# One product of 512 columns for both parts of the activations, and a norm output that is rebuilt

## The chip, the cores and the metric

One core of a Trainium2 chip runs the whole program. Its engines work side by side, each through its own queue in order: TensorE (PE, with PEld for the load of the stationary operand), VectorE (DVE), ScalarE (ACT), GpSimd (POOL), and SyncE (SP), which issues the DMAs. They wait for each other through semaphores. The metric is the device time of one execution in microseconds.

## The reference, cut to what matters

Two layers on 256 tokens of width 1024. Layer 0 mixes tokens by a convolution module, layer 1 by attention; each is followed by an MLP. Every sub-layer starts from a norm with a scale and a shift that come from the conditioning vector c:

```python
h = rms_norm(x, mix_norm_g[i]) * (1.0 + sc1) + sh1
y = conformer_conv(h, ...) if i % 2 == 0 else moba_attention(h, ...)
x = x + g1 * y
h = rms_norm(x, mlp_norm_g[i]) * (1.0 + sc2) + sh2
x = x + g2 * (jnp.square(jax.nn.relu(h @ mlp_w1[i])) @ mlp_w2[i])
```

The hidden width of the MLP is 4096; attention has 16 heads of 64. The modulation vectors (sh, sc, g) are products of silu(c) with ada_w, 6 x 1024 columns for each layer.

## The kernel before, in words

Activations stand transposed: 128 channels on the partitions, 256 tokens along the row, KT = 8 such tiles for the width 1024. Every operand of a large product is kept as two fp32r parts, high and low. For weights, `split` loads 1 MB (`raw`, 5 buffers), rounds it on ACT to `wh`, and subtracts on DVE (in layer 0 a quarter on POOL) to get `wl`; both have 3 buffers. `mm3` then makes a step of three products into the same PSUM region: wh by the high activations, wh by the low ones, wl by the high ones, 256 columns each. A step stands for one tile of 128 output channels and 128 input channels.

The norm is not applied ahead of the products. `norm_prep` stores xT * gm (gm is g * (1 + scale)) in xh and xl, unnormalised. Two more columns (NE = 258) hold the shift, so that a product's column 256 is the shift's share. The token factors `rs_ext` (one over the root mean square) come later, while the products already run, and `evict` multiplies them in when it takes a result out of PSUM; the share of the shift is then added as a bias by ACT (`finish` in the MLP, `squares` and `values` in attention).

An MLP (`mlp(l, slots)`) runs `six` first: w1's blocks b = 0 to 2 (a block is 256 output channels, 16 steps), whose results wait for the token factors. Then come blocks b = 3 to 15, each with `w1_split(b)`, 16 steps and two `finish`. `finish` is a relu and two squares on ACT and one subtraction on DVE into sh and sl. The product with w2 takes 4 column blocks by 4 pieces of the inner width, 16 steps each, and adds the result times the gate to xT on DVE.

The PE's order is written out by hand; short pieces of other work (columns sums, transposes, attention scores) are placed by counting steps (`tick`, `at`). The other engines' queues are set by a scheduler when the program is built: it takes what the program gives it in order, and lets a later instruction pass an earlier one that has to wait. In layer 0 and in the middle of the program DVE also multiplies ada_w by silu(c) (`ada_dve`, `ada_a` in the rows: 4 instructions for each MB of weights).

Attention (`Heads`) takes qkv by blocks of 4 heads, b = 0 to 3, with z = 0, 1, 2 for q, k, v. Block 0 runs in `six`; during block 1 the heads of block 0 go through sums of squares, `norms` (a chain of short DVE instructions that ends with `rb`), `keys` (`kb`, transposes on PE) and the scores.

Of the kernel before, what the change touches and what calls it, by code (L numbers as in the profile page):

```python
# [30 lines left out]
def trunk(ctx, tc, x, c, ada_w, ada_b, mix_g, mlp_g, w_in, b_in, dw, dw_b, ln_g, ln_b, w_out, b_out,
# [123 lines left out]
    xh = const.tile([P, KT, NE], F32R, name="xh")  # L155
    xl = const.tile([P, KT, NE], F32R, name="xl")
    pool.memset(xh[:, :, S:].bitcast(F32), 0.0)
    pool.memset(xl[:, :, S:].bitcast(F32), 0.0)
# [661 lines left out]
    def mlp(l, slots):  # L820

        def fill():
# [3 lines left out]
        with tc.tile_pool(name=f"mlp{l}", bufs=1) as mp:  # L826
            sh = mp.tile([P, FF // P, S], F32R, name="sh")
            sl = mp.tile([P, FF // P, S], F32R, name="sl")
            def finish(ps, f):
# [3 lines left out]
                act.activation(s, t[:, :S], AF.Relu, bias=t[:, S:S + 1])  # L833
                act.activation(sh[:, f, :], s, AF.Square)
                act.activation(s, s, AF.Square)
                dve.tensor_sub(sl[:, f, :], s, sh[:, f, :].bitcast(F32))
# [266 lines left out]
```

## Time and profile before

| what | value |
|---|---|
| median of 3 runs | 672.47 us (672.23 to 672.62) |
| the profiled execution | 670.39 us, its span 668.6 us |
| PE busy | 654.0 us, 98% of the span |
| DVE busy | 494.2 us, 74% |
| ACT busy | 369.2 us, 55% |
| POOL busy | 125.6 us, 19% |
| bytes moved | 150.07 MB, mean 224 GB/s |

The span runs from the first to the last instruction; the profiled execution took 1.8 us more than its span, and 2.1 us less than the median of the runs. PE's busy time is the union of overlapping products whose ends are modelled, so it says where PE had work, not how fast it went. For its speed one reads when products start.

### The profile page before, as it was taken

The page shows a single profiled execution, that of the slowest core. Times are in us where ns is not written, and L with a number is a line of the kernel's source. Part 1 is how long each engine was busy: PE and PEld are TensorE (multiplying, and loading weights), DVE is VectorE, ACT ScalarE, POOL GpSimd, SP SyncE. Part 2 cuts the span into 40 slices and gives each one's busy share as a digit, 9 for nine tenths or more (in the row PEclk, how much of TensorE's full clock was granted, in tenths as well). Part 3 has the DMA queues.
Part 4 walks back from the last instruction along what each step waited for, and adds up shares of the span by engine and source line. Part 5 has one row for each costly group of instructions (what it writes and reads, how often), then busy time and mean ns, then how long its engine had stood idle before and what let it go on. Part 6 is the DMA issues. An engine that isn't in the chain of part 4 may idle for free.

```text
span 668.6 us, 14398 instructions
## 1 busy us (share of the span) xinstructions
PE 654.0 (98%) x5909; PEld 605.2 (91%) x5909; DVE 494.2 (74%) x924; ACT 369.2 (55%) x678; POOL 125.6 (19%) x167
## 2 busy tenths in 40 slices
PE   7899999999999999999999999999999999999997
PEld 6777866699999999999999988988899999999997
DVE  3647993567799999999974998887769986544440
ACT  4537443385877676334443567566668777533330
POOL 5461042302333323345420000000200000000000
PEclk9999999999999999999999999999999999999999
DMA  8998609586479989999994733533356995555300
GB/s 302 340 351 295 240 2 373 216 251 211 151 250 336 346 278 349 342 349 336 349 337 130 237 97 112 181 123 105 101 169 205 334 293 191 186 188 178 110 17 17
DMA packets 107871, 150.07 MB, mean 224 GB/s; under 512 B 2871, under 2 KB 91120, under 8 KB 107806
## 3 DMA queue, kind: packets, MB, share of 16 engines
q1 hardware_dynamic: 107310, 149.04, 66.4%
q8 instruction: 46, 0.75, 0.5%
q14 instruction: 19, 0.16, 0.1%
q0 software_dynamic: 352, 0.07, 0.1%
q10 hardware_dynamic: 144, 0.06, 0.0%
HBM read 148.10 MB, written 1.05 MB: 223 GB/s over the span
## 4 chain that ended last, share of the span: by engine, by line
PE 68%; DVE 21%; issue 4%; ACT 3%; POOL 2%; DMA 2%; SPq 1%; DVEq 0%; ACTq 0%; POOLq 0%
PE m L208 11%; PE m L210 11%; PE m L209 11%; DVE ada_a L301 8%; DVE wl L199 7%; PE qkv L208 4%; PE qkv L209 3%; PE qkv L210 3%; PE cv L403 3%; PE ko L209 2%; PE ko L208 2%; PE ci L208 2%; PE ko L210 2%; PE rep L393 2%; PE ci L210 2%
## 5 line engine op out<-in xcount | busy, mean ns | idle before, releaser
L199 DVE TENSOR_TENSOR wl<-raw,wh 128x1024 fp32r<-128x1024 f32 (+2 forms) x176 | 204.5, 1181 | 59.0 <-ACT wh L196 57.8
L196 ACT CAST wh<-raw 128x1024 fp32r<-128x1024 f32 x176 | 177.7, 1043 | 107.0 <-PE m L209 58.8
L210 PE MATMUL m<-xh,wl 128*128 128x258 f32 x512 | 144.5, 282 | 1.2 <-DVE wl L199 1.1
L208 PE MATMUL m<-sh,wh 128*128 128x256 f32 x512 | 145.4, 284 | 0.0
L210 PE MATMUL m<-sh,wl 128*128 128x256 f32 x512 | 144.3, 282 | 0.8 <-DVE wl L199 0.8
L208 PE MATMUL m<-xh,wh 128*128 128x258 f32 x512 | 145.1, 283 | 0.0
L209 PE MATMUL m<-xl,wh 128*128 128x258 f32 x512 | 144.7, 283 | 0.0
L209 PE MATMUL m<-sl,wh 128*128 128x256 f32 x512 | 144.0, 281 | 0.0
L210 PEld LDWEIGHTS m<-xh,wl 128*128 128x128 f32 x512 | 96.7, 189 | 1.8 <-DVE wl L199 1.8
L208 PEld LDWEIGHTS m<-sh,wh 128*128 128x128 f32 x512 | 96.4, 188 | 1.6 <-issue 0.8
L210 PEld LDWEIGHTS m<-sh,wl 128*128 128x128 f32 x512 | 96.4, 188 | 1.2 <-DVE wl L199 1.2
L208 PEld LDWEIGHTS m<-xh,wh 128*128 128x128 f32 x512 | 96.5, 188 | 1.0 <-issue 0.4
L209 PEld LDWEIGHTS m<-xl,wh 128*128 128x128 f32 x512 | 96.8, 189 | 0.0
L209 PEld LDWEIGHTS m<-sl,wh 128*128 128x128 f32 x512 | 96.4, 188 | 0.0
L201 POOL TENSOR_TENSOR wl<-raw,wh 128x256 fp32r<-128x256 f32 (+1 forms) x60 | 67.7, 1141 | 105.4 <-ACT wh L196 90.7
L301 DVE SCALAR_TENSOR_TENSOR ada_a<-raw,cond,ada_a 128x512 f32<-128x512 f32 x98 | 81.9, 867 | 0.9 <-DMA raw<-in_ada_w_dram 0.7
L208 PE MATMUL qkv<-xh,wh 128*128 128x258 f32 x192 | 56.4, 294 | 0.0
L209 PE MATMUL qkv<-xl,wh 128*128 128x258 f32 x192 | 54.2, 282 | 0.0
L210 PE MATMUL qkv<-xh,wl 128*128 128x258 f32 x192 | 54.1, 282 | 0.0
L833 ACT ACTIVATE s<-tx 128x256 f32<-128x256 f32 x64 | 31.8, 506 | 36.8 <-DVE tx L797 36.7
L730 POOL TENSOR_TENSOR acc<-acc,nsq 128x256 f32<-128x256 f32 x15 | 14.1, 937 | 155.4 <-ACT nsq L728 154.9
L208 PEld LDWEIGHTS qkv<-xh,wh 128*128 128x128 f32 x192 | 36.2, 189 | 4.2 <-issue 4.2
(256 smaller groups left out, 1125.2 us busy)
## 6 DMA issues: line engine op xcount, KB each, us to landing
raw<-in_mlp_w_dram SPq DMA_DIRECT2D x64, 1024.0 KB, 6.7
raw<-in_ada_w_dram SPq DMA_DIRECT2D x46, 1024.0 KB, 7.7
raw<-in_attn_w_qkv_dram SPq DMA_DIRECT2D x12, 1024.0 KB, 6.4
keep<-in_conv_w_in_dram SPq DMA_DIRECT2D x8, 512.0 KB, 9.4
raw<-in_conv_w_in_dram SPq DMA_DIRECT2D x8, 512.0 KB, 5.0
raw<-in_conv_w_out_dram SPq DMA_DIRECT2D x4, 1024.0 KB, 8.1
raw<-in_attn_w_o_dram SPq DMA_DIRECT2D x4, 1024.0 KB, 5.0
early<-in_ada_w_dram SPq DMA_DIRECT2D x2, 1024.0 KB
```

The costliest lines, as they stand in the source:

```text
L196: box["cut"] = [act.copy(wh[:, a:a + n], r[:, a:a + n]).ins]
L199: box["cut"].append(dve.tensor_sub(wl[:, a:m], r[:, a:m], wh[:, a:m].bitcast(F32)).ins)
L201: pool.tensor_tensor(wl[:, m:a + n], r[:, m:a + n], wh[:, m:a + n].bitcast(F32), op=OP.subtract)
L208: pe.matmul(ps, wh, ah, start=start, stop=False, **kw)
L209: pe.matmul(ps, wh, al, start=False, stop=False, **kw)
L210: pe.matmul(ps, wl, ah, start=False, stop=stop, **kw)
L301: dve.scalar_tensor_tensor(a, w, cond[:, k, 0:1], a, op0=OP.mult, op1=OP.add)
L393: pe.matmul(ps[32 * r:32 * r + 32, :284], ident[:, 32 * g:32 * g + 32], UT[i][:, r:r + 284], start=True, stop=True, tile_position=(0, 32 * ...
L403: pe.matmul(ps[32 * g:32 * g + 32, :S], W[:, g, q, :], G[:, g, 4 * q:4 * q + S], start=(q == 0), stop=(q == 7), tile_position=(0, 32 * g))
L730: pool.tensor_tensor(acc, acc, q, op=OP.add)
L833: act.activation(s, t[:, :S], AF.Relu, bias=t[:, S:S + 1])
```

## The change

`mm2` makes a step of two products: wh by both activation parts at once, 512 columns into the two halves of a PSUM bank, and wl by the high part, 256 columns, into the first half. For this the two parts stand side by side: X[0] (`xa`) and a second buffer X[1] (`xb`) replace xh and xl, and `su` replaces sh and sl; the last 8 of the 32 hidden tiles are put into X[0]. It is used for all of w2 in both layers, for w1 of layer 1 from block 5 on (`MERGED = (1,)`), and for qkv from block 1, z = 2 on. Since a product of 512 columns leaves no room for the shift's columns, `whole` rebuilds the norm's output in the other buffer: per tile one DVE product with the token factors, two ACT activations with scale and bias, and one DVE subtraction. It does so at blocks 3 and 4 of w1 in both layers (w1 of layer 0 then runs its blocks from 5 on with three products of 256 columns), and at z = 0 and 1 of attention's block 1. What comes out of a 512-column product is put together by `join`, an ACT copy and a DVE addition; w2's result is added to xT by two DVE instructions instead of one. `finish` and `Heads` leave out the factors and the shift where they are in the operand already.

```diff
+    def mm2(ps, wh, wl, a, start, stop):
+        pe.matmul(ps.rearrange("p (a s) -> p a s", a=2), wh, a, start=start, stop=False, skip_group_check=True)
+        pe.matmul(ps[:, :S], wl, a[:, 0, :], start=False, stop=stop, skip_group_check=True)
+        tick()
...
+    def whole(l, m, i, n):
+        t = work.tile([P, S], F32, name="nsq")
+        dve.tensor_mul(t, xT[:, i, :], rs_ext[:, :S])
+        g, b = gm[:, l, m, i:i + 1], mod[:, l, 3 * m, i:i + 1]
+        act.activation(X[n][:, i, 0, :S], t, AF.Identity, bias=b, scale=g)
+        act.activation(t, t, AF.Identity, bias=b, scale=g)
+        dve.tensor_sub(X[n][:, i, 1, :S], t, X[n][:, i, 0, :S].bitcast(F32))
+
+    def join(ps, t):
+        act.copy(t, ps[:, S:])
+        box["evict"] = dve.tensor_tensor(t, ps[:, :S], t, op=OP.add).ins
...
+                if shifted:
+                    if l in MERGED:
+                        join(ps, t[:, :S])
+                    if l not in MERGED:
+                        act.activation(s, ps[:, :S], AF.Relu)
+                    elif l == 0:
+                        act.activation(s, t[:, :S], AF.Relu)
+                    else:
+                        dve.scalar_tensor_tensor(s, t[:, :S], 0.0, t[:, :S], op0=OP.max, op1=OP.mult)
+                else:
+                    evict(ps, t)
+                    act.activation(s, t[:, :S], AF.Relu, bias=t[:, S:S + 1])
+                u = both(f)
+                if shifted and l == 1:
+                    act.copy(u[:, 0, :], s)
+                else:
+                    act.activation(u[:, 0, :], s, AF.Square)
+                    act.activation(s, s, AF.Square)
+                dve.tensor_sub(u[:, 1, :], s, u[:, 0, :].bitcast(F32))
...
             for b in range(3, FF // 256):
                 with tc.issue_after(box["seam"]) if b > 3 else ExitStack():
                     wh, wl = w1_split(b)
+                if b in (3, 4):
+                    for i in range(4 * b - 12, 4 * b - 8):
+                        whole(l, 1, i, 1)
+                if b == 5:
+                    use(1)
...
+                        if b > 4 and l in MERGED:
+                            mm2(ps, wh[:, o:o + P], wl[:, o:o + P], X[1][:, k, :, :S], k == 0, k == KT - 1)
+                        else:
+                            n = NE if b < 5 else S
+                            mm3(ps[:, :n], wh[:, o:o + P], wl[:, o:o + P], xh[:, k, :n], xl[:, k, :n],
+                                start=(k == 0), stop=(k == KT - 1))
+                    finish(ps, f, b > 4)
...
-                            mm3(ps[j][:, :S], wh[:, o:o + P], wl[:, o:o + P], sh[:, kk, :], sl[:, kk, :],
-                                start=(kk == 0), stop=(kk == FF // P - 1))
+                            mm2(ps[j], wh[:, o:o + P], wl[:, o:o + P], both(kk), kk == 0, kk == FF // P - 1)
...
-                        dve.scalar_tensor_tensor(xT[:, n, :], ps[j][:, :S], mod[:, l, 5, n:n + 1],
-                                                 xT[:, n, :], op0=OP.mult, op1=OP.add)
+                        for h in range(2):
+                            dve.scalar_tensor_tensor(xT[:, n, :], ps[j][:, h * S:h * S + S], mod[:, l, 5, n:n + 1],
+                                                     xT[:, n, :], op0=OP.mult, op1=OP.add)
...
+                if b == 1 and z < 2:
+                    for i in range(4 * z, 4 * z + 4):
+                        whole(1, 0, i, 0)
```

The queues of DVE and ACT come out of the scheduler in a new order. Three places follow; the numbers behind names tell buffers apart and differ between the two programs.

DVE's queue in layer 0's w1, before. The rows `tx_2277` and `tx_2309` take block 3's two results out of PSUM, `tx_2358` and `tx_2390` block 4's, and `wl_2406` is the weight part of block 5:

```order
L797 TENSOR_TENSOR tx_2309<-m1_2284,rs_ext_142 128x258
L299 TENSOR_SCALAR ada_a_2318<-raw_2316,cond_104 128x512 x2
L301 SCALAR_TENSOR_TENSOR ada_a_2318<-raw_2316,cond_104,ada_a_2318 128x512
L836 TENSOR_TENSOR sl_1998<-s2_2279,sh_1997 128x256
L301 SCALAR_TENSOR_TENSOR ada_a_2318<-raw_2316,cond_104,ada_a_2318 128x512
L199 TENSOR_TENSOR wl_2406<-raw_2403,wh_2405 128x768
L836 TENSOR_TENSOR sl_1998<-s2_2311,sh_1997 128x256
L797 TENSOR_TENSOR tx_2358<-m1_2333,rs_ext_142 128x258
L199 TENSOR_TENSOR wl_2406<-raw_2403,wh_2405 128x768
L199 TENSOR_TENSOR wl_2480<-raw_2477,wh_2479 128x768
L797 TENSOR_TENSOR tx_2390<-m1_2365,rs_ext_142 128x258
```

The same place in the changed kernel, from the row that takes out block 4's second result (`tx_2432`) on; `nsq` and `xb` are `whole`'s product and subtraction:

```order
L823 TENSOR_TENSOR tx_2432<-m1_2407,rs_ext_140 128x258
L816 TENSOR_TENSOR xb_1995<-nsq_2355,xb_1995 128x256
L882 TENSOR_TENSOR su_2000<-s2_2332,su_2000 128x256
L812 TENSOR_TENSOR nsq_2370<-xT_137,rs_ext_140 128x256
L312 SCALAR_TENSOR_TENSOR ada_a_2340<-raw_2439,cond_104,ada_a_2340 128x512
L816 TENSOR_TENSOR xb_1995<-nsq_2360,xb_1995 128x256
L312 SCALAR_TENSOR_TENSOR ada_a_2340<-raw_2439,cond_104,ada_a_2340 128x512
L816 TENSOR_TENSOR xb_1995<-nsq_2365,xb_1995 128x256
L312 SCALAR_TENSOR_TENSOR ada_a_2340<-raw_2439,cond_104,ada_a_2340 128x512
L816 TENSOR_TENSOR xb_1995<-nsq_2370,xb_1995 128x256
L312 SCALAR_TENSOR_TENSOR ada_a_2340<-raw_2439,cond_104,ada_a_2340 128x512
L882 TENSOR_TENSOR su_2000<-s2_2401,su_2000 128x256
```

And what stands right behind them, where `wl_2448` is the weight part of block 5:

```order
L312 SCALAR_TENSOR_TENSOR ada_a_2340<-raw_2589,cond_104,ada_a_2340 128x512 x2
L882 TENSOR_TENSOR su_2000<-s2_2433,su_2000 128x256
L204 TENSOR_TENSOR wl_2448<-raw_2445,wh_2447 128x768 x2
L204 TENSOR_TENSOR wl_2520<-raw_2517,wh_2519 128x768 x2
L312 SCALAR_TENSOR_TENSOR ada_a_2340<-raw_2589,cond_104,ada_a_2340 128x512 x2
```

Block 5's weight part has moved from behind block 3's results to behind block 4's, with 14 other instructions between.

ACT's queue at the same place of layer 1 in the changed kernel: `s2_6163` and `s2_6195` are block 4's two results, `wh_6203` is the weight part of block 5, and L814 and L815 are `whole`:

```order
L814 ACTIVATE xb_1995<-nsq_6127,mod_142,gm_143 128x256
L814 ACTIVATE xb_1995<-nsq_6132,mod_142,gm_143 128x256
L815 ACTIVATE nsq_6127<-nsq_6127,mod_142,gm_143 128x256
L815 ACTIVATE nsq_6132<-nsq_6132,mod_142,gm_143 128x256
L875 ACTIVATE s2_6163<-tx_6162 128x256
L875 ACTIVATE s2_6195<-tx_6194 128x256
L880 ACTIVATE su_5773<-s2_6163 128x256
L880 ACTIVATE su_5773<-s2_6195 128x256
L881 ACTIVATE s2_6163<-s2_6163 128x256
L881 ACTIVATE s2_6195<-s2_6195 128x256
L201 CAST wh_6203<-raw_6201 128x1024 x2
L201 CAST wh_6259<-raw_6257 128x1024 x2
```

Before, block 5's weight part (`wh_6490`) went in between block 3's (`s2_6379`, `s2_6411`) and block 4's first result (`s2_6451`):

```order
L833 ACTIVATE s2_6379<-tx_6377 128x256
L196 CAST wh_6490<-raw_6488 128x1024
L834 ACTIVATE sh_6099<-s2_6379 128x256
L833 ACTIVATE s2_6411<-tx_6409 128x256
L835 ACTIVATE s2_6379<-s2_6379 128x256
L834 ACTIVATE sh_6099<-s2_6411 128x256
L196 CAST wh_6490<-raw_6488 128x1024
L835 ACTIVATE s2_6411<-s2_6411 128x256
L833 ACTIVATE s2_6451<-tx_6449 128x256
```

It now waits behind both results of block 4 and behind all 16 activations of `whole`.

DVE's queue in attention around `rb`, which block 0's keys wait for, before; `wl_4979` is the weight part of block 2's q:

```order
L179 SCALAR_TENSOR_TENSOR rsq_t_4727<-rsq_t_4727,vs_4724 128x16
L951 TENSOR_SCALAR q_4894<-tqkv_4757 128x256
L180 SCALAR_TENSOR_TENSOR rsq_y_4726<-rsq_t_4727,rsq_y_4726 128x16
L178 TENSOR_TENSOR rsq_t_4727<-rsq_y_4726 128x16
L199 TENSOR_TENSOR wl_4979<-raw_4976,wh_4978 128x1024
L179 SCALAR_TENSOR_TENSOR rsq_t_4727<-rsq_t_4727,vs_4724 128x16
L199 TENSOR_TENSOR wl_4979<-raw_4976,wh_4978 128x1024
L180 SCALAR_TENSOR_TENSOR rsq_y_4726<-rsq_t_4727,rsq_y_4726 128x16
L797 TENSOR_TENSOR tqkv_4792<-qkv_4767,rs_ext_142 128x258
L971 COPY rb_4740<-rsq_y_4726 128x512
```

The same place in the changed kernel; `xa` and `nsq` are `whole`'s, `tk_4598` is block 1's first k result:

```order
L812 TENSOR_TENSOR nsq_4568<-xT_137,rs_ext_140 128x256
L184 SCALAR_TENSOR_TENSOR rsq_t_4513<-rsq_t_4513,vs_4510 128x16
L816 TENSOR_TENSOR xa_138<-nsq_4558,xa_138 128x256
L185 SCALAR_TENSOR_TENSOR rsq_y_4512<-rsq_t_4513,rsq_y_4512 128x16
L823 TENSOR_TENSOR tk_4598<-qkv_4573,rs_ext_140 128x258
L183 TENSOR_TENSOR rsq_t_4513<-rsq_y_4512 128x16
L1010 TENSOR_SCALAR tq_4492<-tq_4492 128x256
L184 SCALAR_TENSOR_TENSOR rsq_t_4513<-rsq_t_4513,vs_4510 128x16
L1010 TENSOR_SCALAR tq_4543<-tq_4543 128x256
L185 SCALAR_TENSOR_TENSOR rsq_y_4512<-rsq_t_4513,rsq_y_4512 128x16
L816 TENSOR_TENSOR xa_138<-nsq_4563,xa_138 128x256
L1030 COPY rb_4526<-rsq_y_4512 128x512
```

All 16 DVE instructions of `whole` but one stand ahead of `rb`; before, none did, and the two weight parts of block 2's q that stood ahead of `rb` now stand behind it.

## Rows read from the trace of the kernel before

**Rows 1.** Windows by stage (x: instructions; last: granted clock, DMA share, GB/s).

```profile
core 0: us, PE busy (x) PEld busy (x) DVE busy (x) ACT busy (x) POOL busy (x), PEclk, DMA share, GB/s
175.00:253.00 78.00, 76.80 (x642) 75.49 (x644) 75.19 (x119) 57.07 (x110) 23.54 (x24) 1.00 0.87 292
253.00:344.00 91.00, 90.17 (x764) 87.71 (x765) 89.19 (x116) 41.70 (x60) 41.01 (x35) 1.00 1.01 344
...
496.00:571.00 75.00, 75.00 (x632) 74.46 (x631) 62.14 (x101) 60.67 (x118) 0.00 (x0) 1.00 0.75 247
571.00:664.00 93.00, 93.00 (x788) 93.00 (x787) 37.43 (x39) 31.19 (x38) 0.00 (x0) 1.00 0.37 121
```

**Rows 2.** What PE waited for between 175 and 351 us.

```profile
PE m L210 <- DVE wl L199: 1.8, 3, 0.8
```

**Rows 3.** Timeline of PE, four starts of a block (start us, us, engine, ...).

```profile
530.19 0.28 PE L208 MATMUL m<-xh,wh 128*128 128x258 f32 x1
...
553.12 0.28 PE L208 MATMUL m<-xh,wh 128*128 128x258 f32 x1
...
577.23 0.28 PE L208 MATMUL m<-sh,wh 128*128 128x256 f32 x1
...
594.32 0.28 PE L208 MATMUL m<-sh,wh 128*128 128x256 f32 x1
```

**Rows 4.** Timeline of PE: block 5 of w1 starts, layer 0, layer 1.

```profile
186.50 0.28 PE L208 MATMUL m<-xh,wh 128*128 128x258 f32 x1
...
507.26 0.28 PE L208 MATMUL m<-xh,wh 128*128 128x258 f32 x1
```

**Rows 5.** Timeline of DVE, layer 0, after the token factors.

```profile
173.91 1.82 DVE L797 TENSOR_TENSOR tx<-m,rs_ext 128x258 f32<-128x258 f32 x5
...
176.51 0.75 DVE L836 TENSOR_TENSOR sl<-s,sh 128x256 fp32r<-128x256 f32 x2
...
181.31 0.87 DVE L299 TENSOR_SCALAR ada_a<-raw,cond 128x512 f32<-128x512 f32 x2
...
183.58 0.74 DVE L301 SCALAR_TENSOR_TENSOR ada_a<-raw,cond,ada_a 128x512 f32<-128x512 f32 x1
184.25 0.95 DVE L199 TENSOR_TENSOR wl<-raw,wh 128x768 fp32r<-128x768 f32 x1
```

**Rows 6.** Timeline of ACT, layer 1, after the token factors.

```profile
495.03 0.91 ACT L833 ACTIVATE s<-tx 128x256 f32<-128x256 f32 x2 [1.95 <-DVE tx L797]
...
501.13 0.50 ACT L833 ACTIVATE s<-tx 128x256 f32<-128x256 f32 x1
501.53 1.03 ACT L196 CAST wh<-raw 128x1024 fp32r<-128x1024 f32 x1
```

**Rows 7.** Groups of instructions by form, DVE, then ACT (busy us, mean ns).

```profile
L199 DVE TENSOR_TENSOR wl<-raw,wh 128x1024 fp32r<-128x1024 f32 x116 | 141.0, 1236 | 56.0 <-ACT wh L196 54.9
...
L881 DVE SCALAR_TENSOR_TENSOR xT<-m,mod,xT 128x256 f32<-128x256 f32 x16 | 7.7, 478 | 19.8 <-PE m L210 19.8
...
L734 ACT ACTIVATE xh<-xT,gm 128x256 fp32r<-128x256 f32 x24 | 11.9, 496 | 0.0
```

**Rows 8.** Timeline of DVE in attention, from block 0's results to `rb`.

```profile
371.65 0.60 DVE L951 TENSOR_SCALAR q<-tqkv 128x256 f32<-128x256 f32 x2
...
378.27 1.22 DVE L199 TENSOR_TENSOR wl<-raw,wh 128x1024 fp32r<-128x1024 f32 x1
...
381.10 0.41 DVE L971 COPY rb<-rsq_y 128x512 f32<-128x512 f32 x1
```

**Rows 9.** Timeline of PE: the keys of attention's block 0.

```profile
382.06 0.60 PE L991 MATMUL kb<-ident,rb 128*128 128x128 f32 x4
```

**Rows 10.** Timeline of PE at the start and at the end of the program.

```profile
9.21 3.25 PE L320 MATMUL xtp<-ident,xt 128*128 128x128 f32 x16
...
664.72 0.44 PE L861 MATMUL ot<-ident,xT 128*128 128x128 f32 x2 [0.36 <-DVE xT L881]
```

**Rows 11.** Window at the end (columns as in Rows 1).

```profile
667.00:668.60 1.60, 0.00 (x0) 0.00 (x0) 0.00 (x0) 0.00 (x0) 0.00 (x0) 0.58 0.02 4
```

More of the change, by code (lines that the diff above doesn't have):

```diff
@@ L27 @@
 DVE_CONV = (0, 1)
+MERGED = (1,)
 @with_exitstack
@@ L154, in trunk, with use @@
     xT = const.tile([P, KT, S], F32, name="xT")
[L155 to L158, printed above, removed]
+    X = [const.tile([P, KT, 2, NE], F32R, name="xa")]
+    pool.memset(X[0][:, :, :, S:].bitcast(F32), 0.0)
+    xh, xl = X[0][:, :, 0, :], X[0][:, :, 1, :]
+    def use(n):
+        nonlocal xh, xl
+        xh, xl = X[n][:, :, 0, :], X[n][:, :, 1, :]
     rs_ext = const.tile([P, NE], F32, name="rs_ext")
@@ L794, in trunk @@
     cctx.close()
+    X.append(ctx.enter_context(tc.tile_pool(name="xb", bufs=1)).tile([P, KT, 2, NE], F32R, name="xb"))
+    pool.memset(X[1][:, :, :, S:].bitcast(F32), 0.0)
+    def whole(l, m, i, n):
[8 more added lines that the diff above has]
+        box["evict"] = dve.tensor_tensor(t, ps[:, :S], t, op=OP.add).ins
     def evict(ps, t):
@@ L826, in mlp, with both, finish @@
         with tc.tile_pool(name=f"mlp{l}", bufs=1) as mp:
-            sh = mp.tile([P, FF // P, S], F32R, name="sh")
-            sl = mp.tile([P, FF // P, S], F32R, name="sl")
-            def finish(ps, f):
+            su = mp.tile([P, FF // P - KT, 2, S], F32R, name="su")
+            def both(f):
+                n = FF // P - KT
+                return su[:, f] if f < n else X[0][:, f - n, :, :S]
+            def finish(ps, f, shifted=False):
                 t = mp.tile([P, NE], F32, name="tx", bufs=3)
-                evict(ps, t)
                 s = mp.tile([P, S], F32, name="s2", bufs=4)
[L833 to L836, printed above, removed]
+                if shifted:
[17 more added lines that the diff above has]
+                dve.tensor_sub(u[:, 1, :], s, u[:, 0, :].bitcast(F32))
             def w1_split(b):
@@ L914, in trunk @@
             pool.memset(slopes[:, h // 4, h // 2 % 2, :, h % 2], 2.0 ** (-8.0 * (h + 1) / H))
-        oh = ap.tile([P, KT, S], F32R, name="oh")
-        ol = ap.tile([P, KT, S], F32R, name="ol")
+        oh, ol = X[1][:, :, 0, :S], X[1][:, :, 1, :S]
         qt = (slice(0, 128), slice(128, 384))
@@ L942, in squares @@
                 tx = self.tx
-                self.q = [ap.tile([P, S], F32, name="q", bufs=4) for _ in range(2)]
-                self.k = [ap.tile([P, S], F32, name="k", bufs=4) for _ in range(2)]
+                self.q = [tx[0, j][:, :S] for j in range(2)]
+                self.k = [tx[1, j][:, :S] for j in range(2)]
                 self.sq = {}
@@ L949, in squares @@
                         sq = self.sq[2 * z + j] = ap.tile([P, S], F32, name="asq", bufs=4)
-                        act.activation(sq, t[:, :S], AF.Square, bias=t[:, S:S + 1])
-                        dve.tensor_scalar(dst[j], t[:, :S], t[:, S:S + 1], None, op0=OP.add)
+                        if (z, j) in self.shifted:
+                            act.activation(sq, t[:, :S], AF.Square)
+                        else:
+                            act.activation(sq, t[:, :S], AF.Square, bias=t[:, S:S + 1])
+                            dve.tensor_scalar(dst[j], t[:, :S], t[:, S:S + 1], None, op0=OP.add)
             def stats(self):
@@ L980, in values @@
                     t = self.tx[2, j]
-                    v = ap.tile([P, S], F32, name="v", bufs=4)
-                    act.activation(v, t[:, :S], AF.Identity, bias=t[:, S:S + 1])
+                    v = t[:, :S]
+                    if (2, j) not in self.shifted:
+                        act.activation(v, v, AF.Identity, bias=t[:, S:S + 1])
                     for tt in range(2):
@@ L1052, in take, with merged @@
             def take(ps, n):
-                t = hb.tx[n // 2, n % 2] = ap.tile([P, NE], F32, name="tqkv", bufs=8)
-                evict(ps, t)
+                t = hb.tx[n // 2, n % 2] = ap.tile([P, NE], F32, name="t" + "qkv"[n // 2], bufs=6 if n < 4 else 4)
+                if merged():
+                    hb.shifted.add((n // 2, n % 2))
+                    join(ps, t[:, :S])
+                else:
+                    evict(ps, t)
+            def merged():
+                return (b, z) >= (1, 2)
             def qkv_split(z):
                 return split(load(kmajor(w_qkv[0, :, z * D + b * 256:z * D + (b + 1) * 256])), 0, 2)
+            z = 0
             if b == 0:
@@ L1069, in trunk @@
                         o = 256 * k + P * j
-                        mm3(ps[:, :NE], wh[:, o:o + P], wl[:, o:o + P], xh[:, k, :], xl[:, k, :],
-                            start=(k == 0), stop=(k == KT - 1))
+                        if merged():
+                            mm2(ps, wh[:, o:o + P], wl[:, o:o + P], X[0][:, k, :, :S], k == 0, k == KT - 1)
+                        else:
+                            mm3(ps[:, :NE], wh[:, o:o + P], wl[:, o:o + P], xh[:, k, :], xl[:, k, :],
+                                start=(k == 0), stop=(k == KT - 1))
                     take(ps, 2 * z + j)
+        use(0)
         kouter(w_o[0], oh, ol, mod[:, 1, 2, :], 1, 1)
```

6 lines of the change are left out of this document (2 added, 4 removed).

## The prediction

> **What bounds the kernel now.** I read the windows by stage first, then the waits of PE, then the starts of its products, then the queues of DVE and ACT just ahead of the places that the change touches. The reader is to see that PE has work nearly all the time: in both MLPs it is without any for 2.0 us of 337 [rows 1], and of the waits between 175 and 351 us the profile names one kind, three waits of 1.8 us in all for a weight part wl [rows 2]. So the time goes down only if a step gets shorter, and it goes up with every new wait. The second thing to see is how little room the others have: in layer 0 DVE is busy for 75.2 of 78 us in w1 and 89.2 of 91 in w2, where the DMA engines are full too (1.01). In layer 1 DVE has 62.1 of 75 us in w1 and 37.4 of 93 in w2. ACT has room everywhere as a mean [rows 1].
>
> **What a step costs.** Between the two starts at 530.19 and 553.12 lie four blocks of 48 products of 258 columns: 119.4 ns each. Between 577.23 and 594.32 lie 144 products of 256 columns: 118.7 ns each [rows 3]. Two columns cost 0.8 ns, which is 0.4 ns for a column, 2.4 GHz. The columns of one product are then 106.7 ns, and 12.0 ns is a part that does not grow with them. A product of 512 columns is not in the trace. With the fixed part once it takes 225.3 ns, and a step of `mm2` 344.0 ns, against 356.1 for three products of 256 (12.1 less) and 358.2 for three of 258 (14.2 less). I take this, since the two lengths that the trace has differ by just their columns; the ends are 213.3 ns (nothing fixed) and 237.4 (fixed part twice). The page "TensorE: Matmul & The Clock Gate" of the Trainium skill (section "Back-to-back issue gap") puts the fixed part at 2.5 ns; by that rule the merge would spare 2.5 ns a step, about 2 us over the whole program, but the rows show 12.0 here.
>
> **What it gives, by stage.** w1 of layer 1: 11 blocks of 16 steps, 176 x 14.2 = 2.5 us. w2 of layer 1: 256 x 12.1 = 3.1 us. qkv: 7 blocks, 112 x 14.2 = 1.6 us. w1 of layer 0: 176 x 2.4 for the two columns = 0.4 us. w2 of layer 0 would also spare 3.1 us of PE, but there DVE gets eight more instructions of 0.48 us [rows 7] in a stage where it and the DMA are full [rows 1]. At best the stage gains the 3.1 us and PE's 0.8 us of idle time, at worst it loses DVE's 3.8. I take a gain of 1.0, because the blocks before it leave DVE time to get two blocks of weights ahead.
>
> **What `whole` costs: block 5 in layer 0.** The order shows the point on which this forecast rests. The weight part of block 5 stood on DVE behind block 3's results and started at 184.25, in time for PE at 186.50 [rows 4, 5]. Now it stands behind `tx_2432`, which takes out block 4's last result, and that cannot run before PE has finished block 4, at 186.50. PE cannot start block 5 without the weights, so it must stand still while DVE works through what lies between. By the rows a short DVE instruction takes 0.36 us (5 in 1.82), an ada one 0.74 (the first two for a c0 0.44), a weight part 0.95 [rows 5]. DVE begins at 173.91; up to and with `tx_2432` it now has 28 short ones, 4 of ada and one weight part, 13.4 us, until 187.3. Then come 8 short ones, 6 of ada and block 5's first part, 8.3 us: 195.6. With PE's first product, which needs wh alone, 0.2 us are hidden: a wait of 8.9 us. At the least, with DVE free at 186.50, it is 8.4. Behind it the blocks have no `evict` on DVE (22 x 0.36 us less), so the 1.2 us that PE now loses between 175 and 253 [rows 1] do not come again.
>
> **Block 5 in layer 1.** Here ACT is the longer queue. Its weight cast now stands behind 16 activations of `whole` and behind both results of block 4. Three pairs of results took it from 495.03 to 501.13, 2.03 us a pair; two equal activations next to each other take 0.91, so one more costs 0.41 [rows 6] (alone 0.50 [rows 7]). From 501.13 on: two pairs 4.1, `whole` 16 x 0.41 = 6.6, the cast 1.03 [rows 6], then DVE's part 1.24 [rows 7]: 514.1, where PE wants it at 507.26 [rows 4]. Less the 0.2 that is 6.6 us. At the least, with ACT free at 507.26, it is one `evict`, a pair, the cast and the part, 4.5 us. Behind this wait DVE has 6.0 us of `whole` behind it and a `join`, a relu-square and a subtraction for each result; 0.4 us more for each of 22 results makes 62.1 into about 77 us, against some 79 with the wait, so I cost it at nothing, and at up to 3 us if the waits between ACT and DVE add up. The last tile's second addition to xT lies on the path to the end: 0.5 us [rows 7].
>
> **What the waits do to the clock.** The longest stretch in which PE has no work in today's trace is far shorter than these two. At the end, where PE had nothing after 665.2 us, the granted clock of the last 1.6 us is 0.58 of full, so it fell to the lower level, 1.2 GHz; at the start 16 transposes took 3.25 us, 0.20 each, while later four take 0.60 with the modelled end of the last [rows 9 to 11]. So I expect PE to resume at 1.2 GHz after each wait. How long it stays there the trace does not show for this case; by the 3.25 us at the start, and 118.7 ns against 213 for 256 columns, it costs 3.25 x 0.44 = 1.4 us a wait. I take 1.5, ends 0 and 3.3. The same page (section "What you observe") has the fast clock come only after sustained work; on that the trace agrees.
>
> **Attention.** Block 0's `rb` starts at 381.10 and PE takes the keys at 382.06 [rows 8, 9]. Between 371.65 and `rb` 15 short instructions of `whole` come in, 5.4 us; two weight parts of about 1.2 us (the row at 378.27 is one) go behind it, 2.4; the slack is 0.5. That leaves 2.5, or 1.6 where `whole` fills the gaps in the chain of short instructions. I take 2.0, ends 0 and 3.4. ACT has the room.
>
> **The sum.** Layer 0: 8.9 + 1.5 - 0.4 - 1.2 - 1.0 = +7.8. Attention: 2.0 - 1.6 = +0.4. Layer 1: 6.6 + 1.5 - 2.5 - 3.1 + 0.5 = +3.0. Together +11.2 us: the profiled execution would go from 670.4 to 681.6 us. The runs' median is 2.1 us above the profiled one, so I forecast 683.7 us for the median.
>
> **Rivals.** (1) The weight load sets the pace: a product of 256 columns is as long as the load of the next stationary operand, and one of 512 hides it. Then it takes its columns alone, 213.3 ns, and 544 steps outside layer 0's w2 gain 12.0 ns more, 6.5 us: 677.2. Against it: 258 columns take 0.8 ns longer than 256, which a load would not [rows 3]. The page named above (section "LDWEIGHTS (loading the stationary operand)") gives 128 columns 107 ns; by that rule 256 columns would just cover a load. (2) The 512 columns are no cheaper than two products, 237.4 ns: the 6.5 us are lost, 690.2. For it: each fixed part might belong to 256 columns; the rows can't exclude that. (3) The other side: the waits at block 5 do not form, because DVE and ACT are through in time. ACT's 21 us of room in layer 0's w1 speak for it [rows 1]. Without the two waits and their clock (18.5 us) the time is 665.2. The point from which it decides: waits and clock together must stay below 7.3 us. Against it: the order on each queue is fixed, and its least waits, 8.4 and 4.5 us, are above that. (4) Later waits as well, layer 1's w1 bound by DVE (3) and layer 0's w2 at its worst (4.8): 691.5.
>
> **Chances.** My forecast 0.62, rival 1 0.13, rival 2 0.09, rival 3 0.07, rival 4 0.09. The range: without any clock loss (-3), with layer 1's wait at its least (-2.1) and w2 of layer 0 at its best (-2.9) the forecast ends at 675.7; I reach to 675, which takes in rival 1. Upwards it holds rivals 2 and 4 and ends at 693, left out are rival 3 and mixtures. A measurement of this kernel tells from no change what is over about 0.2%, 1.3 us. Slower 0.89; faster 0.08, rival 3 and some of rival 1; same 0.03.
>
> **What would show it.** In the profile of the changed kernel: PE without work for 8 to 9 us ahead of block 5 in layer 0, ended by wl, and for 6 to 7 us in layer 1, with a granted clock below 1 behind each; starts of `mm2`'s products 225 and 119 ns apart; a wait of about 2 us for the keys of block 0; w2 of layer 1 shorter by 3 us, that of layer 0 hardly. The prediction is wrong if block 5 starts on time, or if the 512-column products start less than 205 ns apart (then 544 steps would pay for the rest).

## The result, and the profile after

The changed kernel takes 692.56 us (median of 4 runs, 692.32 to 694.27) against 672.35 for the kernel before on the same chip: a ratio of 1.0317 (95% interval 1.0292 to 1.0342). The direction was forecast. The loss is 20.2 us by the medians and 22.1 us by the two profiled executions, where the sum had 11.2, and by the ratio (693.8 us for a kernel of 672.47) the time lies just above the range's end, 693. The profiled execution took 692.50 us, its span is 690.7.

Where it went, by stage. A stage is counted from PE's first product with wl in it to the next stage's; the starts are 156.22, 253.84, 351.18, 477.21 and 571.33 us before, and 156.24, 264.81, 358.80, 491.68 and 594.46 after.

| stage | before, us | after, us | change | forecast |
|---|---|---|---|---|
| w1, layer 0 | 97.62 | 108.57 | +10.95 | +8.8 |
| w2, layer 0 | 97.34 | 93.99 | -3.35 | -1.0 |
| attention with w_o | 126.03 | 132.88 | +6.85 | +0.4 |
| w1, layer 1 | 94.12 | 102.78 | +8.66 | +5.6 |
| w2, layer 1, to the end of the span | 97.2 | 96.3 | -1.0 | -2.6 |

The windows of the changed kernel (columns as in [rows 1]) show the three places where PE stands still, and what its clock did behind each:

```profile
186.00:194.00 8.00, 1.47 (x9) 1.03 (x7) 8.00 (x19) 8.00 (x19) 0.70 (x1) 0.76 0.52 146
194.00:204.00 10.00, 7.97 (x37) 7.61 (x37) 8.54 (x10) 5.49 (x8) 9.39 (x6) 0.51 0.57 198
204.00:264.00 60.00, 60.00 (x509) 59.32 (x511) 54.97 (x75) 41.74 (x82) 27.89 (x20) 1.00 0.99 339
264.00:358.00 94.00, 94.00 (x564) 80.34 (x567) 86.68 (x114) 39.69 (x55) 39.56 (x53) 1.00 0.97 331
408.00:412.00 4.00, 1.18 (x13) 0.93 (x10) 3.03 (x14) 0.37 (x1) 0.00 (x0) 1.00 0.74 259
412.00:416.00 4.00, 4.00 (x18) 3.49 (x16) 2.27 (x4) 3.02 (x5) 0.00 (x0) 0.58 0.22 89
522.00:529.00 7.00, 0.17 (x1) 0.17 (x1) 3.62 (x10) 7.00 (x16) 0.00 (x0) 0.69 0.00 0
529.00:535.00 6.00, 5.54 (x17) 4.36 (x18) 5.58 (x5) 4.51 (x5) 0.00 (x0) 0.51 0.45 137
```

From 194 to 204 us PE makes 37 products where at the full clock some 84 would fit, at a granted clock of 0.51; from 204 on the clock is 1.00 again. What PE waited for, in three stretches (150 to 350, 350 to 495, 488 to 690 us; [rows 2] had one kind, 1.8 us):

```profile
PE m L213 <- ACT wh L201: 6.5, 1, 6.5
PE m L215 <- DVE wl L204: 1.1, 1, 1.1
PE m L215 <- POOL wl L206: 0.9, 1, 0.9
...
PE kb L1051 <- DVE ws L1033: 3.1, 2, 2.8
PE ko L787 <- DVE tv L820: 1.2, 1, 1.2
PE kb L1051 <- DVE rb L1030: 1.0, 1, 1.0
...
PE m L220 <- ACT wh L201: 6.9, 1, 6.9
PE ot L916 <- DVE xT L936: 1.0, 1, 1.0
PE m L221 <- DVE wl L204: 0.5, 1, 0.5
```

The starts of PE's products answer to [rows 3, 4, 9]: the two waits at block 5, products at the lower clock (198.77 to 203.46, 531.11 to 534.31), block 1's keys (411.17), and seven blocks of merged steps (543.53 to 582.54):

```profile
186.46 0.28 PE L215 MATMUL m<-xa,wl 128*128 128x258 f32 x1
193.27 0.58 PE L213 MATMUL m<-xb,wh 128*128 128x256 f32 x1 [6.53 <-ACT wh L201]
...
195.19 0.58 PE L215 MATMUL m<-xb,wl 128*128 128x256 f32 x1 [1.13 <-DVE wl L204]
...
198.77 0.42 PE L213 MATMUL m<-xb,wh 128*128 128x256 f32 x1
...
203.46 0.41 PE L214 MATMUL m<-xb,wh 128*128 128x256 f32 x1
...
411.17 0.63 PE L1051 MATMUL kb<-ident,rb 128*128 128x128 f32 x4 [2.82 <-DVE ws L1033]
...
521.67 0.28 PE L215 MATMUL m<-xa,wl 128*128 128x258 f32 x1
528.83 0.80 PE L220 MATMUL m<-xb,wh 128*128 128x512 f32 x1 [6.88 <-ACT wh L201]
530.09 0.58 PE L221 MATMUL m<-xb,wl 128*128 128x256 f32 x1 [0.46 <-DVE wl L204]
...
531.11 0.63 PE L220 MATMUL m<-xb,wh 128*128 128x512 f32 x1
...
534.31 0.63 PE L220 MATMUL m<-xb,wh 128*128 128x512 f32 x1
...
543.53 0.28 PE L221 MATMUL m<-xb,wl 128*128 128x256 f32 x1
...
582.54 0.28 PE L221 MATMUL m<-xb,wl 128*128 128x256 f32 x1
```

Between 543.53 and 582.54 lie 112 steps, 348.3 ns each, where I took 344.0. ACT in layer 1 answers to [rows 6]: from 515.66 it works without a gap on `whole` and block 4's results until block 5's cast at 527.75. The first two rows are those of block 2's results, for the length of an activation.

```profile
513.63 0.90 ACT L875 ACTIVATE s<-tx 128x256 f32<-128x256 f32 x2
514.43 0.71 ACT L880 ACTIVATE su<-s 128x256 fp32r<-128x256 f32 x2
...
515.66 1.08 ACT L814 ACTIVATE xb<-nsq,mod,gm 128x256 fp32r<-128x256 f32 x2
516.65 1.09 ACT L815 ACTIVATE nsq<-nsq,mod,gm 128x256 f32<-128x256 f32 x2
517.63 1.17 ACT L814 ACTIVATE xb<-nsq,mod,gm 128x256 fp32r<-128x256 f32 x2
...
527.75 5.76 ACT L201 CAST wh<-raw 128x1024 fp32r<-128x1024 f32 x6
```

In attention the place is block 1's chain on DVE, not block 0's of [rows 8]: from `vs` to `rb` it takes 7.3 us, and three weight parts (L204) stand in it:

```profile
403.27 0.17 DVE L1025 TENSOR_SCALAR vs<-stt 128x16 f32<-128x16 f32 x1
403.35 1.21 DVE L204 TENSOR_TENSOR wl<-raw,wh 128x1024 fp32r<-128x1024 f32 x1
...
404.56 1.22 DVE L204 TENSOR_TENSOR wl<-raw,wh 128x1024 fp32r<-128x1024 f32 x1
...
407.33 1.22 DVE L204 TENSOR_TENSOR wl<-raw,wh 128x1024 fp32r<-128x1024 f32 x1
...
410.60 0.43 DVE L1030 COPY rb<-rsq_y 128x512 f32<-128x512 f32 x1
```

Before, the same chain took 5.7 us with two of them in it, and PE came 0.16 us before it was done (DVE, then PE of the kernel before):

```profile
393.43 0.17 DVE L966 TENSOR_SCALAR vs<-stt 128x16 f32<-128x16 f32 x1
...
399.11 0.43 DVE L971 COPY rb<-rsq_y 128x512 f32<-128x512 f32 x1
```

```profile
399.68 0.63 PE L991 MATMUL kb<-ident,rb 128*128 128x128 f32 x4 [0.16 <-DVE ws L974]
```

### The profile page after: what moved, and what is told of

Same layout as the page of the kernel before. It is cut to its first block, busy times and chain, and to the rows that moved or that the text cites. A ratio compares the mean times of both kernels' runs of the same rounds, so it can differ in the third digit from the quotient of the medians.

```text
span 690.7 us, 12867 instructions
## 1 busy us (share of the span) xinstructions
PE 654.2 (95%) x5109; PEld 568.3 (82%) x5109; DVE 513.6 (74%) x980; ACT 378.8 (55%) x712; POOL 136.9 (20%) x167
## 4 chain that ended last, share of the span: by engine, by line
PE 82%; ACT 7%; DVE 4%; POOL 2%; DMA 2%; issue 1%; SPq 1%; DVEq 0%; ACTq 0%; POOLq 0%
PE m L220 23%; PE m L221 12%; PE m L213 5%; PE m L215 5%; PE m L214 5%; PE qkv L220 3%; PE cv L414 3%; PE ko L214 2%; PE ko L213 2%; PE ci L213 2%; PE ko L215 2%; PE rep L404 2%; PE ci L215 2%; PE qkv L221 2%; PE ci L214 2%; DMA keep<-in_conv_w_in_dram 2%
## 5 line engine op out<-in xcount | busy, mean ns | idle before, releaser
L204 DVE TENSOR_TENSOR wl<-raw,wh 128x1024 fp32r<-128x1024 f32 (+2 forms) x176 | 205.3, 1186 | 63.3 <-ACT wh L201 63.2
L220 PE MATMUL m<-su,wh 128*128 128x512 f32 x384 | 136.1, 398 | 0.0
L221 PE MATMUL m<-su,wl 128*128 128x256 f32 x384 | 106.9, 278 | 0.0
L220 PEld LDWEIGHTS m<-su,wh 128*128 128x128 f32 x384 | 72.1, 188 | 17.9 <-issue 0.8
L221 PEld LDWEIGHTS m<-su,wl 128*128 128x128 f32 x384 | 72.3, 188 | 0.0
L220 PE MATMUL m<-xb,wh 128*128 128x512 f32 x176 | 63.9, 405 | 6.9 <-ACT wh L201 6.9
L213 PE MATMUL m<-xb,wh 128*128 128x256 f32 x176 | 51.4, 292 | 6.5 <-ACT wh L201 6.5
L215 PE MATMUL m<-xb,wl 128*128 128x256 f32 x176 | 51.7, 294 | 2.0 <-DVE wl L204 1.1
L214 PE MATMUL m<-xb,wh 128*128 128x256 f32 x176 | 51.3, 291 | 0.0
L221 PE MATMUL m<-xb,wl 128*128 128x256 f32 x176 | 50.5, 287 | 0.5 <-DVE wl L204 0.5
L220 PEld LDWEIGHTS m<-xb,wh 128*128 128x128 f32 x176 | 34.4, 195 | 15.2 <-ACT wh L201 7.1
L213 PE MATMUL m<-xa,wh 128*128 128x258 f32 x160 | 45.6, 285 | 0.0
L214 PE MATMUL m<-xa,wh 128*128 128x258 f32 x160 | 45.5, 284 | 0.0
L220 PE MATMUL m<-xa,wh 128*128 128x512 f32 x128 | 45.2, 395 | 0.0
L213 PEld LDWEIGHTS m<-xb,wh 128*128 128x128 f32 x176 | 35.2, 200 | 7.2 <-ACT wh L201 6.7
```

Source lines behind the costliest of these rows:

```text
L204: box["cut"].append(dve.tensor_sub(wl[:, a:m], r[:, a:m], wh[:, a:m].bitcast(F32)).ins)
L220: pe.matmul(ps.rearrange("p (a s) -> p a s", a=2), wh, a, start=start, stop=False, skip_group_check=True)
L221: pe.matmul(ps[:, :S], wl, a[:, 0, :], start=False, stop=stop, skip_group_check=True)
```

## The experiments

The profiled executions differ in the part that no experiment touches: w1 of layer 0 starts between 155.9 and 159.1 us. So beside the times stand the stages, start to start as in the table above (w2 of layer 1: its first fifteen blocks of sixteen). Each time is a median; the ratios below are to the kernel before, run on the same chip. Of each edit the lines that matter are shown.

| kernel | time, us | w1, 0 | w2, 0 | attention | w1, 1 | w2, 1 |
|---|---|---|---|---|---|---|
| before | 671.6 to 672.4 | 97.62 | 97.34 | 126.03 | 94.12 | 87.19 |
| changed | 692.56 | 108.57 | 93.99 | 132.88 | 102.78 | 85.71 |
| 1, w2 alone | 671.60 | 97.73 | 98.16 | 125.86 | 94.31 | 86.05 |
| 2, attention before | 685.90 | 108.72 | 94.00 | 125.93 | 103.50 | 85.68 |
| 3, three products | 698.00 | 108.31 | 96.63 | 131.57 | 103.71 | 87.84 |
| 4, filler | 692.17 | 108.34 | 93.99 | 132.88 | 100.65 | 85.71 |
| 5, no whole in layer 0 | 686.96 | 97.75 | 98.04 | 133.92 | 103.60 | 85.68 |
| 6, whole spread | 678.40 | 103.27 | 96.01 | 125.97 | 95.70 | 85.67 |
| 7, whole, no merge in attention | 691.70 | 107.73 | 94.00 | 131.10 | 103.68 | 85.68 |
| 8, merge, no whole in attention | 688.68 | 108.54 | 94.00 | 128.07 | 101.88 | 85.70 |
| 9, keys later | 690.80 | 108.82 | 93.99 | 129.25 | 103.01 | 85.71 |
| 10, w2 placed, three products | 674.03 | 97.86 | 98.87 | 125.88 | 94.31 | 87.19 |
| 11, w2 alone, parts apart | 671.95 | 97.77 | 98.03 | 125.87 | 94.31 | 86.05 |
| 12, w2 of layer 1 alone | 670.69 | 97.74 | 96.42 | 125.89 | 94.31 | 86.20 |

**1, w2 alone.** w1, norm and attention as before (`whole`, `join` and the other merged steps are out), w2 as changed:

```diff
-            su = mp.tile([P, FF // P - KT, 2, S], F32R, name="su")
+            su = mp.tile([P, FF // P, 2, S], F32R, name="su")
...
```

> Only w2 of both layers is merged (mm2, su with all 32 hidden tiles); w1, attention and the norm are as before, whole and join are gone. In the changed kernel a step of mm2 starts 348 ns after the one before it (356 before), and w2 took 3.3 us less in layer 0 and 1.6 less in layer 1. Theory A, the steps themselves give that in both layers: 672.4 - 3.3 - 1.6 = 667.5 us. Theory B, layer 0's 3.3 us came only because the long wait at block 5 gave DVE and the DMAs time to get ahead, and DVE's eight more additions eat the gain there: 672.4 - 1.6 = 670.8 us.

671.60 against 671.55 us, ratio 1.0007 (0.9994 to 1.0020): no difference. Layer 0's w2 is not shorter but 0.8 us longer, so B holds there. In layer 1 the fifteen blocks are 1.14 us shorter, 4.8 ns a step (steps start 351.0 ns apart), and the last addition takes back about half a microsecond.

**2, attention before.** qkv with 258 columns throughout, no `whole` there, and the two activation buffers in swapped roles in layer 1:

```diff
-                if b == 1 and z < 2:
-                    for i in range(4 * z, 4 * z + 4):
-                        whole(1, 0, i, 0)
...
-                return (b, z) >= (1, 2)
+                return False
...
```

> The changed kernel with attention's products as before (no whole, no 512-column product in qkv; the two activation buffers change roles in layer 1). Theory A, what I forecast at +0.4 us and the trace shows as +6.9 us is made by whole in attention and the waits behind it: 692.6 - 6.9 = 685.7 us, and the waits of 1.1 us for rb and 2.8 us for ws are gone. Theory B, whole costs only the one wait for rb that I forecast (and the merge gives 0.9 us back); the rest comes from DVE being late when it enters attention or from the shared buffers: 692.6 - 0.4 = 692.2 us, with a wait for ws still there.

685.90 us (ratio 1.0222, 1.0199 to 1.0244), the stage at 125.93: A. All 6.9 us come from the change in attention, none from what DVE brought along from before it.

**3, three products.**

```diff
-        pe.matmul(ps.rearrange("p (a s) -> p a s", a=2), wh, a, start=start, stop=False, skip_group_check=True)
+        pe.matmul(ps[:, :S], wh, a[:, 0, :], start=start, stop=False, skip_group_check=True)
+        pe.matmul(ps[:, S:], wh, a[:, 1, :], start=False, stop=False, skip_group_check=True)
```

> The changed kernel with each 512-column product made as two of 256 into the same two halves; all else is the same, 800 steps. Theory A, the 512-column product costs what the starts in the changed kernel's trace show (steps of 348.4 ns against 356.1): 800 x 7.7 ns = 6.2 us more, 698.8 us. The forecast's 225.3 ns for 512 columns: 800 x 12.1 = 9.7 us more, 702.3 us. Theory B, 512 columns are no cheaper than two products (rival 2): 692.6 us.

698.00 us (1.0390, 1.0372 to 1.0409), 5.4 us more than the changed kernel. Rival 2 is out. In layer 1's w2 the fifteen blocks lose 2.13 us, 8.9 ns a step. Attention is 1.3 us shorter in spite of its longer steps: PE waits 2.4 us instead of 2.8 for block 1's keys, and the granted clock stays at 1.00 behind that wait. In layer 0's w2, with the same long wait ahead of it as in the changed kernel, three products take 96.63 us where the merged steps take 93.99.

**4, filler.**

```diff
+                    for _ in range(FILL[l] if b == 5 and j == 0 else 0):
+                        pe.matmul(ps[:, :S], X[0][:, 0, 0, :P], X[0][:, 1, 0, :S], start=True, stop=True, skip_group_check=True)
```

> The changed kernel with extra products ahead of block 5 of w1 (56 in layer 0, 58 in layer 1, about 119 ns each, into a bank that the next product clears), so that PE works where it stood still; the wait for the weights is not shortened. Theory A, the lower granted clock behind each wait is a cost of its own: with the clock kept at full, block 5 gives back 3.9 us in layer 0 and 2.5 in layer 1: 692.6 - 6.4 = 686.2 us. Theory B, in layer 0 DVE and POOL are behind anyway, so a faster PE only waits for the next weight parts: -2.5 from layer 1 alone, 690.1 us. Theory C, the clock does not depend on what PE did: 692.6 us.

692.17 us, 0.4 us below the changed kernel with runs that overlap, so the stages of the two profiles decide. Windows of this kernel, to be set beside those after the change:

```profile
186.00:194.00 8.00, 7.61 (x65) 7.21 (x63) 8.00 (x19) 8.00 (x19) 0.66 (x1) 1.00 0.52 144
194.00:204.00 10.00, 7.05 (x38) 6.75 (x39) 8.55 (x10) 5.52 (x8) 9.42 (x6) 0.66 0.60 200
522.00:529.00 7.00, 6.68 (x57) 6.25 (x55) 3.61 (x10) 7.00 (x16) 0.00 (x0) 1.00 0.00 0
529.00:535.00 6.00, 5.24 (x31) 4.54 (x31) 6.00 (x7) 4.54 (x6) 0.00 (x0) 1.00 0.50 149
```

The clock follows what PE does, so C is out. In layer 1 it stays at 1.00 and w1 is 2.13 us shorter. In layer 0 PE still waits 3.1 us for the next weight parts (wl from POOL 1.7, from DVE 1.4), the clock falls there, and the stage is 0.2 us shorter: B.

**5, no whole in layer 0.**

```diff
-                if b in (3, 4):
+                if l and b in (3, 4):
...
```

> The changed kernel with w1 of layer 0 as before (258 columns, no whole); w2 of both layers, attention and layer 1 are as changed, with the two activation buffers in swapped roles. Theory A, in layer 0's w2 DVE and the DMAs set the pace, so the 3.3 us that it was shorter came from the long wait ahead of it and go with it: layer 0 then costs 0.9 us against before, as in the kernel with w2 alone, where the changed kernel loses 7.6 there: 692.4 - 6.7 = 685.7 us. Theory B, w2's gain is the merged steps' own and stays: 692.4 - 11.2 = 681.2 us.

686.96 us (1.0230, 1.0209 to 1.0251): A, 1.3 us beside it. w1 is back at 97.75, and w2 goes back to 98.04: without the wait ahead of it the merged steps gain nothing there. With the wait they do, as experiment 3 shows (96.63 against 93.99), so the 3.35 us need both.

**6, whole spread.** Attention as in 2.

```diff
-                if b in (3, 4):
-                    for i in range(4 * b - 12, 4 * b - 8):
+                if 4 <= b < 8:
+                    for i in range(2 * b - 8, 2 * b - 6):
...
-                if b == 5:
+                if b == 9:
...
```

> Attention as before (685.9 us), and in both MLPs whole is spread: two tiles at each of blocks 4 to 7, first use at block 9, where it was four tiles at blocks 3 and 4 and first use at block 5. The work is the same. Theory A, the waits come from the crowding of whole between block 4's results and block 5's weights: the waits at block 5 (9.1 and 7.9 us) and the low clock behind them (3.9 and 2.5) go; layer 0 keeps 0.9 us, layer 1 loses 0.6 us of merge (64 steps of 9.8 ns): 685.9 - 6.7 - 10.4 + 0.6 = 669.4 us. Theory B, DVE has no room for whole in layer 0 wherever it stands, so its 16 short instructions (5.8 us) come back as many small waits there: 675 us.

678.40 us (1.0102, 1.0080 to 1.0123), above both. In layer 1 the wait and the low clock are gone, 103.50 to 95.70 us. In layer 0 one large wait became several (150 to 357 us):

```profile
PE m L215 <- DVE wl L204: 6.3, 5, 2.0
PE m L221 <- DVE wl L204: 1.5, 1, 1.5
```

DVE is busy for 97.78 of 103 us there, so the 16 instructions of `whole` have no place: B. By stages, against experiment 2, layer 0 gives back 3.4 us (B had 0.9) and layer 1 gives 7.8 (both theories had 9.8), and w1 of layer 0 starts 3.2 us later in this profile. Layer 1's w1 is still 1.6 us longer than before. At five places there a weight part from DVE comes late (product starts at 516.43, 521.15, 534.43, 561.92 and 563.72), and the ten steps at them take 1.9 us more than their like; the profile calls only 0.3 us of it a wait.

**7, whole without the merge, and 8, the merge without whole**, in attention. 7 is 2 with `whole` kept; 8 keeps the merge and leaves out the lines of `whole`:

```diff
-                if b == 1 and z < 2:
-                    for i in range(4 * z, 4 * z + 4):
-                        whole(1, 0, i, 0)
```

> Attention's products as before, but whole is done at block 1 all the same and its result is not used. Without whole the time was 685.9 us; the changed kernel has 692.4 with 112 merged steps that give about 1 us back, so whole, join and the waits behind them cost 7.5 to 8. Theory A, whole's 16 DVE and 16 ACT instructions make DVE late for the rest of the attention: 685.9 + 7 = 692.9 us, with waits for rb and ws. Theory B, whole's delay is worked off after the one wait for rb and the joins (an ACT copy and a DVE addition that hold each bank longer) make the rest: 685.9 + 1.5 = 687.4 us.

> The changed kernel without whole in attention: the merged products from block 1's v on take what the other buffer holds (hidden values of the MLP), so what is computed is not attention of the norm; all instructions but whole's 48 are there. Theory A, whole is the price: about 692.4 - 7 = 685.4 us and no wait for ws. Theory B, the joins are the price: 692.4 - 1.5 = 690.9 us, with the wait for ws still there.

691.70 us (1.0297, 1.0274 to 1.0320) and 688.68 us (1.0251, 1.0229 to 1.0273). By stage `whole` alone costs 131.10 - 125.93 = 5.2 us and the merge alone 2.1. Neither theory holds by itself: `whole` is the larger part, but the merge, which I had put down as a gain of 1.6, loses too. PE's waits in attention with `whole` alone, then with the merge alone:

```profile
PE kb L1051 <- DVE ws L1033: 2.4, 1, 2.4
PE kb L1051 <- DVE rb L1030: 1.0, 1, 1.0
```

```profile
PE ko L787 <- DVE tv L820: 1.2, 1, 1.2
...
PE kb L1051 <- DVE ws L1033: 0.8, 2, 0.5
```

The wait for tv belongs to `join`: w_o's bank comes free only when a result has been through ACT and DVE, where `evict` was one instruction. In the changed kernel the copy starts at 457.54, behind a weight cast, and the addition at 458.81, behind a weight part.

**9, keys later** (block 1's row of the table of places):

```diff
-                      (9, 12, 18, 31, 47, (37, 47), (60, 79), (66, 85)),
+                      (9, 12, 18, 40, 47, (45, 51), (62, 79), (68, 85)),
```

> The changed kernel with block 1's keys placed 9 steps (3.1 us) later in PE's order, its two scores 8 and 4 steps later and the turn and product of the first pair 2 steps later. Theory A, the attention's loss is a wait at one place that had no slack (PE was there 0.2 us ahead of DVE in the kernel before): with PE coming 3 us later the 2.8 us go and the lower clock behind them (about 1.8 us) too: 692.4 - 4.6 = 687.8 us. Theory B, DVE is behind in the whole rest of the attention, so the wait turns up at the scores, turns or products that follow: at least 690.5 us.

690.80 us (1.0277, 1.0251 to 1.0302); the time alone is nearer to B. The stage is 3.6 us shorter, with the clock at 1.00 between 412 and 416 us, while w1 of layer 0 starts 1.5 us later in this profile than in the changed kernel's. The wait for ws shrank and did not go:

```profile
PE kb L1051 <- DVE ws L1033: 1.6, 2, 1.4
```

So most of A holds: PE came to a place without slack. But DVE ends its chain later as well.

**10 and 11, where the parts lie.** 10 is 1 with the edit of 3; 11 is 1 with

```diff
-            su = mp.tile([P, FF // P, 2, S], F32R, name="su")
+            su = mp.tile([P, 2, FF // P, S], F32R, name="su")
...
```

> Only w2's operands are placed as in the change (the two parts of a hidden tile side by side), but each 512-column product is two of 256. Theory A, the placement itself costs: in layer 1's w2 a step of three takes 358.6 ns, as in the changed kernel with three products, against 356.1 in the kernel before; so merging is worth 358.6 - 351 = 7.6 ns there and 2.5 of it go into the placement. Theory B, the placement costs nothing, 356.1 ns; the 358.6 came from the rest of the changed kernel.

> Only w2 is merged, in both layers, with all high parts first and then all low parts in the buffer; the 512-column product takes its two halves from two places 32 tiles apart. Theory A, the placement side by side costs 2.5 ns a step: 348.4 instead of 351 ns in layer 1's w2, 671.6 - 0.7 = 670.9 us. Theory B, it does not matter where the halves lie: 351 ns, 671.6 us.

B in both. Three products with the parts side by side start 118.6 ns apart in layer 1's w2 (674.03 us, 1.0029, 1.0009 to 1.0049), and with the parts apart a merged step takes the same 351 ns (671.95 us, 1.0011, 0.9996 to 1.0026). So merging is worth 4.8 ns a step in these kernels and 8.9 in the changed one, and whether the parts lie side by side does not explain the difference. The traces show what goes with it, the buffer: in layer 1's w2 of experiment 3 a step of three products takes 358.7 to 360.0 ns on the 24 tiles in `su` and 355.1 on the 8 in X[0], of the changed kernel's merged ones 348.9 to 350.2 and 350.4. Merging is worth some 9.9 ns in `su` and 4.7 in X[0]. Why a buffer matters stays open.

**12, w2 of layer 1 alone**, the one part that gained:

```diff
+                            one = l == 0 or (b, j) == (3, 1)
...
+                            if one:
+                                mm3(ps[j][:, :S], wh[:, o:o + P], wl[:, o:o + P], u[:, 0, :], u[:, 1, :], *e)
...
```

> The kernel before with w2 of layer 1 merged and nothing else (parts apart, the last of the eight output tiles with three products and one addition). Layer 0's w2, which DVE and the DMAs bound, is as before. Theory A, 224 steps give 7.7 ns each: 1.7 us less than the kernel before, a ratio of 0.9975. Theory B, 5 ns each, as in the kernel with w2 alone: 1.1 us less, 0.9983. Both lie near what a measurement can tell.

670.69 us, 0.9988 (0.9972 to 1.0004): the sign of B, not to be told from no change. w2 of layer 1 is 1.0 us shorter. No kernel here beats the one before by more than the measurement can tell.

## Why the prediction was half right

**Layer 0, block 5 (forecast 8.9 + 1.5): right in place and length, but most of the wait was ACT's.** The wait is 193.27 - 186.58 = 6.7 us for wh (at 186.58 the next product would have started), 1.3 for wl and 1.1 for POOL's quarter, 9.1 in all. The chain through DVE ended where I had it: PE's first product with wl starts at 195.19, and I had 195.6. But the sum followed DVE alone. ACT, whose 21 us of room spoke for rival 3, is busy for all 8 us from 186 to 194, and its chain ended only 1.9 us ahead of DVE's; so the sign that I named, a wait of 8 to 9 us ended by wl, was not seen. POOL's quarter I had not followed either. The low clock took 3.9 us of block 5's 12.0, where I had 1.5. Experiment 4 got 0.2 of it back, since a faster PE met the next late weights, and the clock fell there; what a full clock throughout would be worth in layer 0 is not shown. The stage lost 2.2 us more than forecast.

**Layer 0, w2 (-1.0).** Experiments 1 and 5: merged, it gains nothing (98.0 to 98.2 us, before 97.3; 98.9 with three products, 96.4 in experiment 12 with one addition, so it varies by a microsecond among kernels). There DVE and the DMAs set its pace, as [rows 1] said. In the changed kernel the long wait has let them get ahead: PE has work for 94.00 of 94 us, and the stage takes 93.99 to 94.00 us in all six kernels that have both the wait and the merge, 96.63 with the wait and three products. So the merge is worth 2.6 us here, but only behind a wait that costs more. That the stage gave more than forecast hides 2.4 us of what the others lost.

**Attention (+0.4): the step that failed.** "I take 2.0" looked at one chain, that of block 0, which cost 1.0. I did not ask where DVE would be 20 us later: it is busy for 15.7 of the 16 us from 392 to 408 (before, 15.3 of those from 384 to 400), so the delay is still there when block 1's chain comes up, at a place where PE had waited 0.16 us even before. Counted from the stage's start, the chain starts 2.2 us later than before and is 1.6 us longer, by the third weight part in it; PE comes 1.2 us later. The wait is 2.8 us, the clock of the next four microseconds 0.58 (some 1.7 us), w_o's bank 1.2 late. And the 1.6 us that the merge was to give were a loss: experiments 7 and 8 put 5.2 us on `whole` and 2.1 on the merge. This is 6.5 of the 10.9 us by which the sum fell short of the 22.1 of the profiles.

**Layer 1, w1 (6.6 + 1.5 - 2.5): right mechanism, three sizes off.** The wait is 7.9 us, 7.04 for wh and 0.83 for wl: ACT's chain stood as I wrote it, but an activation of `whole`, with a scale and a bias as operands, took 0.49 us next to its like, and not the 0.41 of a relu with a bias alone (a square with neither takes 0.31); 16 x 0.08 = 1.3. The clock cost 2.1 (experiment 4), not 1.5: I took the time at the lower clock, 3.25 us, from the start of the program, and here it lasted 6.0 us after PE resumed. And the merged step took 348.3 ns, not 344.

**The 512-column product (225.3 ns).** A step is 348 to 352 ns by kernel and stage, so 512 columns cost some 229 to 234, between my value and the end of 237.4. In w1 of layer 1 the buffer goes with it again: 348.3 ns where the steps read X[1] (changed kernel, 4, 8, 9), mostly 352.5 where they read X[0] (2, 5, 6, 7). 240 steps of layer 1's w2 gave 1.48 us where the forecast's 12.1 ns would give 2.9. Rival 1 is out, rival 2 too; rival 3, that the waits don't form, is what experiment 6 shows for layer 1 once `whole` is spread, and even then the stage does not win. Rival 4's 691.5 is near the measured time by coincidence: layer 0's w2 became shorter, not longer, layer 1's w1 had no later waits, and the later waits that came were in attention, where it had none.

## What to carry to other kernels

A few instructions on a full engine can be paid for again at a later place where another engine arrives without slack, as long as the full engine has had no idle time; so follow the delay to the next such place and the one after, not only to the first. A stage that another engine or the DMAs bound turns time lost ahead of it into a shorter stage, so read gains there only with the wait removed. And 5 to 9 ns a step don't pay for waits: the 240 steps of layer 1's w2 gave 1.5 us, one wait in attention took 2.8 and the clock behind it almost two more.
